# RWKV-7 scan: triangular inverses from 16 x 16 blocks on GpSimd and two block levels on TensorE, in place of 32 x 32 blocks and one level

## The chip, the core and the metric

One core of a Trainium2 chip runs the whole program in one launch. The metric is the device time of one execution in microseconds; the kernel before was executed three times.

## What is computed

The program is a two-layer trunk over 512 latent and 256 context tokens of width 1024. Layer 0 is half-SwiGLU, HGRN2 mixer, half-SwiGLU; layer 1 is half-SwiGLU, RWKV-7 mixer, half-SwiGLU; a final RMSNorm ends it. The change is in the RWKV-7 mixer of layer 1, in the scan over tokens. The reference, cut to that scan:

```
def rwkv_scan(decay, k, v, kk, b, r, s0, reverse):        # 16 heads of 64, two directions
    def step(s, inp):
        dec, kt, vt, kkt, bt = inp[:5]
        sa = einsum('bhvk,bhk->bhv', s, kkt)
        s = s * dec[:, :, None, :] - sa[..., None] * bt[:, :, None, :] + vt[..., None] * kt[:, :, None, :]
        y = einsum('bhvk,bhk->bhv', s, inp[5]) if with_out else None
        return s, y
```

Context tokens come first in each direction, and the latent scan starts from the final context state of the same direction.

## The kernel before, in words

`rwkv_scan(l)` (L1180) works in chunks of 64 tokens. In a chunk the recurrence becomes (I + A) U = right-hand side with a strictly triangular 64 x 64 matrix A for each head and direction, so each chunk needs the inverse Y of I + A; then come the products with U. A **group** is four heads (two channel tiles `e`, the half `hp` of each), both directions `d`, four chunks: 32 matrices of 64 x 64. There are 4 quads of heads times 3 groups (one of context, two of latent tokens), 12 in all, in the list `todo`.

For a group these generators write the instructions:

- `prep_a` (L1224) loads the features, makes the decays, forms A by products on TensorE (L1303), masks it on VectorE into `N` (L1309), transposes the backward one (`NT_`, L1314), and writes the diagonal blocks of 32 x 32 to a DRAM tile `md`, 8 DMAs on SyncE's queue (L1317): four from `N`, four from `NT_`.
- `prep_m` (L1322) loads `md` by GpSimd's queue so that each of 64 partitions holds one block (L1329), inverts all 64 blocks at once in 30 steps of two operations on GpSimd, a product into `mt` (L1335) and a sum into `M` (L1336), sets the diagonal (L1338) and writes the DRAM tile `me` (L1339).
- `prep_d` (L1343) reads `me` back into `P1`, blocks at their place in 64 columns, 8 DMAs on SyncE's queue (L1349).
- `prep_b` (L1351) turns k and b to tokens-major and forms A V (`bkt`, `W`).
- `prep_c` (L1385) transposes `P1` (L1390, two operations on VectorE) and forms the one off-diagonal 32 x 32 block of each matrix by two products of 32 x 32, `TT` (L1408) and `Yo` (L1410), with an eviction between them (L1413) and four copies behind (L1420, L1422).
- `scan` (L1429) runs the four chunks one after the other: `kG`, `rhs`, `U`, `VU`, `G`, and `y` on latent groups. `readout` (L1496) closes a quad.

Each matrix product of float32 shows as two MATMUL rows in the trace.

While group i is scanned, the loop at the end writes into the same stream the steps of `prep_a` of group i+2, of `prep_d`, `prep_b` and `prep_c` of group i+1, and of the inversions, at rates per step of the scan (`RP`, `RM`, `RO`). `SEQ = 'Adabc'` sets the order: two steps of `prep_a`, then `prep_d`, then the rest of `prep_a`, then b and c:

```
parts = {"A": islice(ahead, 2), "a": ahead, "b": stage(prep_b, i + 1), "c": ..., "d": urgent(stage(prep_d, i + 1), HP[2])}
prep = chain(*(parts[x] for x in SEQ))
for _ in urgent(scan(*k, *ready.pop(k)), HP[0]):
    for n, (f, r) in enumerate(((inversions, RM), (prep, RP), (out, RO))):
```

A scheduler then fixes the order on each engine and on each queue from an estimate of the times, with priorities from `urgent`; on the chip each engine and SyncE's queue go in that order and wait for what is not there yet. Tiles of 1024 floats come from two rotating sets, `Q` (L1191): 13 for `KR`, `BK`, `Ar`, 15 (`NQ2`) for the rest, `M` among them. PSUM banks come from `bank` (L1197).

Of the kernel before, what the change touches and what calls it, by code (L numbers as in the profile page):

```python
# [26 lines left out]
NQ1, NQ2 = 13, 15  # L27
RM, RP, RO, RV, RF = 3.0, 5.0, 0.3, 1.5, 1.3
# [25 lines left out]
# columns of the packed per-channel vectors  # L54
# [14 lines left out]
NCST = 790  # L69
# [4 lines left out]
def trunk(ctx, tc, io, phases=None, dump=None):  # L74
# [58 lines left out]

    def urgent(gen, by):
        """the steps of gen, their instructions ahead of others that wait"""
# [7 lines left out]
    def both(*gens):  # L143
        """the steps of all, in turns"""
# [31 lines left out]
    def wunit(src, nk, n=128, lo_on=None, keep=False):  # L176
        """[nk*128, n] of DRAM (or several, side by side) -> two parts whose sum it is, [128, nk, n] each"""
# [18 lines left out]
    def weights(todo, depth=None):  # L196
        """the units of todo in turn, those after them on their way"""
# [12 lines left out]
    def mm3_steps(p, w, c0, xs, n, cols=None):  # L210
        """p[:, :n] = (whi+wlo)[:, k, c0:c0+128]^T (xhi+xlo)[:, :n], summed over k; cols: (from, to, where in p) of other columns"""
# [31 lines left out]
    def mod_steps(l, s, ws=None, alloc=psmall):  # L243
        """part s of 9: [128, tile 8, (lat, ctx)]"""
# [32 lines left out]
    def rsqrt(p, n, scale, eps, lowest=None):  # L277
        """(scale*p + eps)^-0.5 of the n columns of p, to float32's accuracy"""
# [17 lines left out]
    def spread(ys, n, alloc=psum):  # L296
        """[128 tokens, chunk] -> the tokens along the free axis, on every partition (PSUM)"""
# [5 lines left out]
    def sums(x, n):  # L303
        """sum over the partitions of x[:, t] -> PSUM [128 tokens, chunk]"""
# [5 lines left out]
    def square(j, n, acc):  # L310
        """acc + h_j^2"""
# [15 lines left out]
    def norm_steps(l, sub, rs, out):  # L327
        """the modulated norm of h, in two parts, a tile at a time"""
# [80 lines left out]
        # sh, its upper half less its lower one, in two parts, and zeros  # L409
# [87 lines left out]
    def ffn(l, w, n, prep, fill=iter(()), rate=0.5):  # L497
        """prep: what is left of blocks' steps; fill: other work for the tensor engine, rate steps of it per unit of weights.
        Stops before the last rows; the steps that remain are two for each tile of the residual."""
# [44 lines left out]
        def columns(f):  # L544
            """g of the tile f"""
# [47 lines left out]
        def rows(f0, gs):  # L593
            """the residual from the tiles f0.. of g"""
# [41 lines left out]
    def hand_over(rest, prep):  # L636
        """the last rows of an FFN; what comes next prepares from each tile of the residual as it is done"""
# [10 lines left out]
    def lower_bound():  # L648
        """(lb, 1-lb): [128, dir*8+head]; softmax over the layers, of which there is one"""
# [13 lines left out]
    def hgrn(l, extra, after, u1, parts, cols, normed):  # L663
        """extra: for each head, parts of the modulation to work out on the way; after: steps to take as the residual's
        tiles are done"""
# [35 lines left out]
        def project(hd, first=False):  # L701
            F = pair("F")      # [bwd, fwd]
# [74 lines left out]
    def hgrn_head(hd, F, K2, qa, vals, ys):  # L777
# [35 lines left out]
        # products of the decays of blocks of 2, 4, ... 128 tokens  # L813
# [42 lines left out]
        # states at the head of each chunk  # L856
# [53 lines left out]
    def rwkv_dense(l, xpool, root):  # L910
        """all but the values that comes before the scan, per token; results go to DRAM"""
# [23 lines left out]
        def neighbour(j):  # L935
            """neighbour less token"""
# [25 lines left out]
        def mix_halves(m, n, out, low):  # L962
            """two steps for each tile"""
# [14 lines left out]
        def products(n):  # L978
            """n tiles for products; of one bank, there are the others"""
# [6 lines left out]
        def part(out, w, x, k, nk=NT):  # L986
            """the share of the input tile k in a product: out, a list of (PSUM, columns of the weights, from, to)"""
# [5 lines left out]
        # the first half of r and the hidden layers of a and of the decay, an input tile at a time: they come in one by one  # L993
# [78 lines left out]
        def features():  # L1072
            for j in range(NT):
# [49 lines left out]
                # output gate  # L1123
# [5 lines left out]
                # input of the values  # L1129
# [632 lines left out]
```

## Time and profile before

| what | value |
|---|---|
| three executions | 3957.18, 3948.7, 3953.75 us (median 3953.75) |
| span of the profiled execution | 3956.9 us (of the three executions the nearest took 3957.18 us) |
| TensorE busy | 3574.5 us, 90% |
| VectorE busy | 2687.5 us, 68% |
| ScalarE busy | 1454.9 us, 37% |
| GpSimd busy | 1424.3 us, 36% |
| granted TensorE clock, mean | 0.922 |

How to read it: TensorE is busy for 90% of the whole, but the share is a mean over stages. Clock 1.0 in a row is 2.4 GHz, 0.5 is 1.2 GHz, and a number between them is a mean over a stretch that had both. "PE" is TensorE's products, "DVE" VectorE, "ACT" ScalarE, "POOL" GpSimd, "SPq" SyncE's DMA queue. Times in rows are from the start of the span. A row's bracket tells how long the engine sat idle before it and what ended the wait.

### The profile page before, as it was taken

What the parts mean: (1) busy time and instruction counts of PE and PEld (TensorE: products, weight loads), DVE (VectorE), ACT (ScalarE), POOL (GpSimd) and SP (SyncE); (2) the same over time, 40 slices, a digit from 0 to 9 for tenths busy, and PEclk for the clock granted to TensorE, in tenths of its full rate; (3) what the DMA queues carried; (4) which work ended last, traced back from release to release, by engine and by line L of the source; (5) the groups of instructions that cost most, each with busy time, mean ns of one, the idle gap of its engine ahead of it and who ended that gap; (6) DMA issues with size and microseconds to landing.
All of it is one profiled execution on the core that took longest, in us unless ns stands there. A gap on an engine that the chain in (4) does not pass through costs nothing. (4 is left out here: it accounts for less than half of the span.)

```text
span 3956.9 us, 62237 instructions
## 1 busy us (share of the span) xinstructions
PE 3574.5 (90%) x24898; PEld 3201.7 (81%) x24898; DVE 2687.5 (68%) x4187; ACT 1454.9 (37%) x2168; POOL 1424.3 (36%) x1395
## 2 busy tenths in 40 slices
PE   4999999799999799999899999689878888888998
PEld 3999997688888699999799999566767776668887
DVE  7777676766576777767777677677444554468886
ACT  5433333432333544333533333344322222234343
POOL 3222223343343421222422222522356766623332
PEclk7999999999999899999999999799967777779999
DMA  5333232321111233333233222247632332232332
GB/s 162 107 96 101 86 91 64 89 61 41 41 49 38 59 106 114 107 102 107 64 94 91 83 89 90 64 133 228 189 92 69 90 84 66 60 104 82 98 93 80
DMA packets 517056, 362.56 MB, mean 92 GB/s; under 512 B 83517, under 2 KB 490333, under 8 KB 516766
## 3 DMA queue, kind: packets, MB, share of 16 engines
q1 hardware_dynamic: 513694, 350.19, 30.3%
q0 software_dynamic: 1920, 6.29, 0.6%
q8 instruction: 196, 3.21, 0.4%
q10 hardware_dynamic: 1152, 2.10, 0.2%
q14 instruction: 94, 0.77, 0.1%
HBM read 315.64 MB, written 42.87 MB: 91 GB/s over the span
## 5 line engine op out<-in xcount | busy, mean ns | idle before, releaser
L550 POOL TENSOR_TENSOR raw<-raw 128x512 f32<-128x512 f32 x88 | 132.5, 1506 | 1406.7 <-DMA raw<-in_ffn_w_in 797.8
L606 PE MATMUL po<-g,whi 128*128 128x512 f32 (+1 forms) x2464 | 585.3, 348 | 6.6 <-ACT g L207 4.0
L533 PE MATMUL c<-u,whi 128*128 128x386 f32 (+1 forms) x2112 | 521.9, 331 | 59.6 <-DVE uu L564 18.1
L192 ACT ACTIVATE whi<-raw 128x1024 fp32r<-128x1024 f32 (+1 forms) x337 | 335.0, 1000 | 401.8 <-PE po L606 122.8
L525 ACT ACTIVATE whi<-raw 128x1024 fp32r<-128x1024 f32 x352 | 330.6, 949 | 413.1 <-PE po L606 151.9
L526 DVE TENSOR_TENSOR wlo<-raw,whi 128x1024 fp32r<-128x1024 f32 x352 | 424.9, 1217 | 75.4 <-ACT whi L525 28.9
L606 PEld LDWEIGHTS po<-g,whi 128*128 128x128 f32 x2464 | 402.6, 189 | 69.9 <-ACT g L207 4.8
L533 PEld LDWEIGHTS c<-u,whi 128*128 128x128 f32 x2112 | 371.6, 190 | 74.5 <-ACT u L445 31.2
L193 DVE TENSOR_TENSOR wlo<-raw,whi 128x1024 fp32r<-128x1024 f32 (+1 forms) x289 | 358.8, 1248 | 57.8 <-ACT whi L192 56.4
L533 PE MATMUL a<-u,whi 128*128 128x386 f32 (+1 forms) x1408 | 349.3, 331 | 24.3 <-DVE u L427 14.8
L606 PE MATMUL po<-g,wlo 128*128 128x512 f32 (+1 forms) x1232 | 361.4, 347 | 0.0
L610 DVE SCALAR_TENSOR_TENSOR h<-po,mod,h 128x512 f32<-128x512 f32 (+1 forms) x384 | 226.9, 627 | 189.5 <-PE po L606 189.2
L533 PE MATMUL b<-u,whi 128*128 128x386 f32 (+1 forms) x1408 | 343.2, 328 | 3.5 <-ACT pp L561 2.2
L533 PE MATMUL c<-u,wlo 128*128 128x386 f32 (+1 forms) x1056 | 344.5, 326 | 0.0
L533 PEld LDWEIGHTS a<-u,whi 128*128 128x128 f32 x1408 | 252.1, 193 | 28.6 <-DVE u L427 15.3
L533 PEld LDWEIGHTS b<-u,whi 128*128 128x128 f32 x1408 | 246.2, 190 | 6.3 <-ACT pp L561 3.0
L533 PE MATMUL b<-u,wlo 128*128 128x386 f32 (+1 forms) x704 | 229.9, 327 | 4.2 <-DVE wlo L526 4.1
L533 PE MATMUL a<-u,wlo 128*128 128x386 f32 (+1 forms) x704 | 232.5, 330 | 0.5 <-DVE wlo L526 0.5
L606 PEld LDWEIGHTS po<-g,wlo 128*128 128x128 f32 x1232 | 205.9, 189 | 30.3 <-DVE wlo L193 0.2
L193 POOL TENSOR_TENSOR wlo<-raw,whi 128x1024 fp32r<-128x1024 f32 x48 | 126.4, 2634 | 278.6 <-ACT whi L192 269.3
L1335 POOL TENSOR_TENSOR mt<-M 64x168 f32<-64x168 f32 (+5 forms) x360 | 191.2, 532 | 66.9 <-DMA M<-md 34.7
L1336 POOL TENSOR_TENSOR M<-M,mt 64x168 f32<-64x168 f32 (+5 forms) x360 | 200.4, 557 | 26.4
(365 smaller groups left out, 7607.9 us busy)
## 6 DMA issues: line engine op xcount, KB each, us to landing
raw<-in_ffn_w_in SPq DMA_DIRECT2D x176, 512.0 KB
raw<-in_mod_w SPq DMA_DIRECT2D x144, 512.0 KB
raw<-in_ffn_w_out SPq DMA_DIRECT2D x80, 384.0 KB
raw<-in_hgrn_w_in SPq DMA_DIRECT2D x40, 512.0 KB
raw<-in_ffn_w_out SPq DMA_DIRECT2D x28, 512.0 KB
raw<-in_w_rkv SPq DMA_DIRECT2D x24, 512.0 KB
ld<-s_bk SPq DMA_DIRECT2D x48, 256.0 KB
s_bk<-knb SPq DMA_DIRECT2D x32, 192.0 KB
```

The lines of the kernel that those rows point to most:

```text
L192: act.activation(hi[:, :m], raw[:, :m], AF.Copy)
L193: (lo_on or slots["lo"]).tensor_tensor(lo[:, :m], raw[:, :m], hi[:, :m].bitcast(F32), ALU.subtract)
L525: act.activation(hi, x, AF.Copy)
L526: dve.tensor_tensor(lo, x, hi.bitcast(F32), ALU.subtract)
L533: pe.matmul(p[:, :q], a[:, c], x[k][:, b], start=first and k == 0 and i == 0, stop=k == 3 and i == 2, skip_group_check=not first)
L550: pool.tensor_tensor(S[:, lo], U[:, lo], U[:, hi], ALU.add)
L606: pe.matmul(p[v][:, :t1 - t0], wx[:, k, at:at + 128], x[:, e, t0:t1], start=k == 0 and i == 0, stop=k == nk - 1 and i == 2)
L610: dve.scalar_tensor_tensor(h[d][:, t0:t1], p[v][:, :t1 - t0], mods[l, sub, 2][:, d, v:v + 1], h[d][:, t0:t1], ALU.mult, ALU.add)
L1335: eng.tensor_tensor(t, M[:, 0:j, j:j + 1].to_broadcast([64, j, n]), M[:, j:j + 1, j + 1:32].to_broadcast([64, j, n]), ALU.mult)
L1336: eng.tensor_tensor(M[:, 0:j, j + 1:32], M[:, 0:j, j + 1:32], t, ALU.add)
```

## The change: what it does

The diagonal blocks become 16 x 16, so a group has 128 of them and fills 128 partitions; the inversion has 14 steps in place of 30. The blocks come back into `X` ([128, 2, 2, 8, 32]), a compact layout of 32 columns. `prep_c` gets a level more: with `T16` and `R16`, 64 products of 32 x 32 each, it makes 32 x 32 inverses from 16 x 16 ones, the old level follows on `A` and its transpose `AT`, and the result stands in `Y`. A mask `off16` comes with the constants. The steps of the inversions per step of the scan go from 3.0 to 1.5, `NQ2` from 15 to 14. Comments are taken out elsewhere. The core of the diff:

```diff
-NQ1, NQ2 = 13, 15
-RM, RP, RO, RV, RF = 3.0, 5.0, 0.3, 1.5, 1.3
+NQ1, NQ2 = 13, 14
+RM, RP, RO, RV, RF = 1.5, 5.0, 0.3, 1.5, 1.3
...
-        diagonal = [[B1.tile([128, 16, 64], F32, name=f"P1_{i}{d}") for d in range(2)] for i in range(2)]
+        diagonal = [B1.tile([128, 2, 2, 8, 32], F32, name=f"X16_{i}") for i in range(2)]
+        whole = [B1.tile([128, 2, 8, 64], F32, name=f"Y_{i}") for i in range(2)]
...
-        lanes = [(d, hp, b, d * 32 + (hp * 2 + b) * 8, 64 * hp + 32 * b) for d in range(2) for hp in range(2) for b in range(2)]
+        lanes = [(d, hp, b, d * 64 + (hp * 4 + b) * 8, 64 * hp + 16 * b) for d in range(2) for hp in range(2) for b in range(4)]
...
             for d, hp, b, l0, r0 in lanes:
                 nc.sync.dma_start(out=md[l0:l0 + 8].rearrange("l s t -> s l t"),
-                                  in_=(N[0] if d == 0 else NT_)[r0:r0 + 32, 8 * hp:8 * hp + 8, 32 * b:32 * b + 32])
+                                  in_=(N[0] if d == 0 else NT_)[r0:r0 + 16, 8 * hp:8 * hp + 8, 16 * b:16 * b + 16])
...
-            M = Q("M")[0:64, :1024].rearrange("l (s t) -> l s t", t=32)
+            M = B1.tile([128, 16, 16], F32, tag="M", name="M", bufs=2)
...
-            for j in range(30, 0, -1):
-                n = 31 - j
+            for j in range(14, 0, -1):
+                n = 15 - j
                 t = mt[:, :j * n].rearrange("l (a b) -> l a b", b=n)
-                eng.tensor_tensor(t, M[:, 0:j, j:j + 1].to_broadcast([64, j, n]), M[:, j:j + 1, j + 1:32].to_broadcast([64, j, n]), ALU.mult)
-                eng.tensor_tensor(M[:, 0:j, j + 1:32], M[:, 0:j, j + 1:32], t, ALU.add)
+                eng.tensor_tensor(t, M[:, 0:j, j:j + 1].to_broadcast([128, j, n]), M[:, j:j + 1, j + 1:16].to_broadcast([128, j, n]), ALU.mult)
+                eng.tensor_tensor(M[:, 0:j, j + 1:16], M[:, 0:j, j + 1:16], t, ALU.add)
...
             for d, hp, b, l0, r0 in lanes:
-                nc.sync.dma_start(out=P1[d][r0:r0 + 32, 8 * hp:8 * hp + 8, 32 * b:32 * b + 32], in_=me[l0:l0 + 8].rearrange("l s t -> s l t"))
+                o = 16 * (b % 2)
+                nc.sync.dma_start(out=X[r0:r0 + 16, d, d, :, o:o + 16], in_=me[l0:l0 + 8].rearrange("l s t -> s l t"))
...
-            for d in range(2):
-                dve.transpose(PT[d], P1[d][:, :, :32 + 32 * d])
+            for d in range(2):
+                dve.transpose(X[:, 1 - d, d].rearrange("p s n -> p (s n)"), X[:, d, d].rearrange("p s n -> p (s n)"))
...
+            p = view(bank("T16"))
+            for d in range(2):
+                for c in range(8):
+                    for hp, b, a in rows32:
+                        pe.matmul(p[a:a + 32, d, c], N[d][a:a + 32, 8 * hp + c, 32 * b:32 * b + 32], X[a:a + 32, 1, d, c], start=True, stop=True, tile_position=(a, a))
+                yield
+            dve.tensor_tensor(t16.rearrange("p d s n -> p (d s) n"), p.rearrange("p d s n -> p (d s) n"), off16.unsqueeze(1).to_broadcast([128, 16, 32]), ALU.mult)
+            p = view(bank("R16"))
+            for d in range(2):
+                for c in range(8):
+                    for hp, b, a in rows32:
+                        pe.matmul(p[a:a + 32, d, c], t16[a:a + 32, d, c], X[a:a + 32, 0, d, c], start=True, stop=True, tile_position=(a, a))
+                yield
+            A, AT = tile_of("A32"), tile_of("AT32")
+            dve.tensor_tensor(flat(A), flat(X[:, 0]), flat(p), ALU.add)
+            dve.transpose(flat(AT), flat(A))
+            for hp, b, a in rows32:
+                act.activation(Y[a:a + 32, :, :, 32 * b:32 * b + 32], A[a:a + 32], AF.Copy)
...
-                                    other = (PT[0] if d == 0 else P1[1])[a:a + 32, s, ca:ca + 32]
-                                    pe.matmul(pt[b:b + 32, lo:lo + 32], N[d][a:a + 32, s, cb_:cb_ + 32], other, start=True, stop=True, tile_position=(a, b))
+                                pe.matmul(pt[b:b + 32, lo:lo + 32], N[d][a:a + 32, 8 * hp + c, 32 * (1 - d):32 * (1 - d) + 32], AT[a:a + 32, d, c], start=True, stop=True, tile_position=(a, b))
...
-                        pe.matmul(p[half(hp), at(d, e)], Y[d][half(hp), slot(hp, e, cs[d])], rhs[half(hp), at(d, e)], start=True, stop=True)
+                        pe.matmul(p[half(hp), at(d, e)], Y[half(hp), d, 4 * e + cs[d]], rhs[half(hp), at(d, e)], start=True, stop=True)
```

## Rows read from the trace of the kernel before

**Rows 1.** The page's chain that ended last, over the whole run: shares of the span by engine.

```profile
PE 14%; POOL 4%; DVE 3%; DMA 1%; issue 1%; ACT 0%; SPq 0%; POOLq 0%; ACTq 0%; DVEq 0%
```

**Rows 2.** Busy time in the stretch of the scan's loop. Columns: from:to, length, then PE, PEld, DVE, ACT, POOL busy us (instructions), granted clock, DMA share, GB/s.

```profile
2870.00:3440.00 570.00, 476.10 (x6473) 402.25 (x6471) 270.05 (x601) 141.31 (x340) 369.42 (x695) 0.74 0.30 76
```

**Rows 3.** GpSimd's instructions in order of time: its loads of the blocks, the write of the inverses, the first of the 60 operations between them, and a pair of them.

```profile
2903.75 0.52 POOL L1329 DMA_DIRECT2D M<-md  x1 [32.58 <-PE Yo L1410]
...
2992.04 0.52 POOL L1329 DMA_DIRECT2D M<-md  x1 [10.12 <-DMA hw_s<-s_hw]
...
3301.36 0.52 POOL L1329 DMA_DIRECT2D M<-md  x1 [9.45 <-ACT Ei L1266]
3305.00 0.26 POOL L1335 TENSOR_TENSOR mt<-M 64x30 f32<-64x30 f32 x1 [3.12 <-DMA M<-md]
3305.34 0.26 POOL L1336 TENSOR_TENSOR M<-M,mt 64x30 f32<-64x30 f32 x1
...
3342.68 0.59 POOL L1339 DMA_DIRECT2D me<-M  x1 [0.29 <-POOL M L1336]
3353.18 0.52 POOL L1329 DMA_DIRECT2D M<-md  x1 [9.91 <-DMA md<-NT]
3398.38 0.52 POOL L1329 DMA_DIRECT2D M<-md  x1 [3.00 <-PE kG L1446]
```

**Rows 4.** SyncE's queue in order of time in the same turn, issue time of so many DMAs.

```profile
3345.60 3.75 SPq L1349 DMA_DIRECT2D P<-me  x8
3349.45 1.88 SPq L1317 DMA_DIRECT2D md<-NT  x4
```

**Rows 5.** The longest waits of SyncE's queue from 2870 to 3500: us in total, times, longest.

```profile
SPq L1349 <- DMA me<-M: 142.6, 12, 30.5
SPq L1242 <- PE y L1483: 49.0, 5, 15.9
```

**Rows 6.** Busy time from one load of blocks to the next, groups 3 to 11 (columns as in rows 2; the last row is the sum).

```profile
3045.26:3088.29 43.03, 42.43 (x603) 34.97 (x600) 23.10 (x53) 13.14 (x33) 33.69 (x64) 0.80 0.33 90
3088.29:3142.30 54.01, 42.41 (x534) 35.60 (x530) 25.00 (x56) 11.09 (x27) 33.83 (x63) 0.66 0.33 79
...
sum 406.34, PE 350.28 PEld 293.23 DVE 208.36 ACT 104.51 POOL 271.76; mean PE 43.79 PEld 36.65 DVE 26.05 ACT 13.06 POOL 33.97
```

**Rows 7.** Waits from 2870 to 3500, of VectorE and of TensorE: us in total, times, longest; and TensorE's two waits for the first transpose with their places.

```profile
DVE PT L1390 <- DMA P<-me: 89.7, 13, 15.9
...
PE TT L1408 <- DVE PT L1390: 25.1, 4, 13.1
PE U L1455 <- DVE rhs L1448: 14.1, 10, 5.5
...
PE cum L1263 <- DVE sg L1254: 7.7, 1, 7.7
PE sw L1250 <- DVE Ar L1309: 7.1, 1, 7.1
...
2956.91 0.31 PE L1408 MATMUL TT<-PT,N 32*32 32x32 f32 x4 [13.06 <-DVE PT L1390]
...
3403.56 0.32 PE L1408 MATMUL TT<-PT,N 32*32 32x32 f32 x4 [5.83 <-DVE PT L1390]
```

**Rows 8.** GpSimd's operations by shape, 3000 to 3040: busy us, mean ns of one, idle before.

```profile
L1335 POOL TENSOR_TENSOR mt<-M 64x240 f32<-64x240 f32 x2 | 1.6, 776 | 0.2
...
L1336 POOL TENSOR_TENSOR M<-M,mt 64x58 f32<-64x58 f32 x1 | 0.3, 279 | 0.0
L1335 POOL TENSOR_TENSOR mt<-M 64x30 f32<-64x30 f32 x1 | 0.2, 230 | 0.1
```

**Rows 9.** Pieces of the chain (start us, us, what) with the 32 x 32 products: a piece between others, an unbroken run at full clock, one at half clock; then the busy time of the instructions of `TT`, and of `Yo`, in the stretch of groups 3 to 11 (columns as in rows 2, engines that have none left out: PE, PEld and ACT for `TT`).

```profile
3360.84 0.17 PE TT L1408 x2
...
3364.26 0.70 PE Yo L1410 x50
...
3448.84 1.08 PE Yo L1410 x64
...
2992.04:3398.38 406.34, 17.61 (x512) 11.20 (x512) 3.07 (x8) 0.75 0.31 78
...
2992.04:3398.38 406.34, 10.88 (x512) 8.34 (x512) 6.61 (x16) 6.02 (x16) 0.75 0.31 78
```

**Rows 10.** Operations of VectorE and ScalarE by shape, 2992 to 3399: busy us, mean ns of one, idle before.

```profile
L1390 DVE STREAM_TRANSPOSE PT<-P 128x1024 f32<-128x1024 f32 x8 | 9.9, 1237 | 0.0
...
L1390 DVE STREAM_TRANSPOSE PT<-P 128x512 f32<-128x512 f32 x7 | 5.0, 711 | 50.9 <-DMA P<-me 50.9
...
L1507 DVE SCALAR_TENSOR_TENSOR ybuf<-mean,ybuf 128x512 f32<-128x512 f32 x5 | 3.4, 681 | 1.0 <-PE mean L1506 1.0
...
L1367 ACT ACTIVATE BKT<-bkt 128x512 f32<-128x512 f32 x33 | 19.0, 598 | 13.6 <-PE bkt L294 10.0 <-POOL M L1336 3.4
```

**Rows 11.** Busy time and granted clock in stretches of 4 us (columns as in rows 2).

```profile
3184.00:3188.00 4.00, 0.00 (x0) 0.00 (x0) 0.00 (x0) 0.00 (x0) 0.00 (x0) 0.89 0.40 81
3188.00:3192.00 4.00, 1.48 (x4) 1.19 (x5) 2.98 (x6) 0.00 (x0) 0.00 (x0) 0.50 0.33 51
...
3204.00:3208.00 4.00, 4.00 (x72) 3.08 (x72) 1.91 (x9) 0.00 (x0) 3.45 (x8) 0.95 0.00 0
3208.00:3212.00 4.00, 4.00 (x63) 3.28 (x63) 0.42 (x1) 0.50 (x2) 3.53 (x7) 0.50 0.02 4
```

More of the change, by code (lines that the diff above doesn't have):

```diff
@@ L68 @@
 NV = V_C + 16
-NCST = 790
+NCST = 822
 @with_exitstack
@@ L1210, in decay_weights @@
             nc.sync.dma_start(out=w2[64:65], in_=io["w0"][:, 256 * qd:256 * qd + 256].unsqueeze(0))
-        diagonal = [[B1.tile([128, 16, 64], F32, name=f"P1_{i}{d}") for d in range(2)] for i in range(2)]
-        for d in range(2):
-            dve.memset(diagonal[0][d], 0.0)
-            pool.memset(diagonal[1][d], 0.0)
+        diagonal = [B1.tile([128, 2, 2, 8, 32], F32, name=f"X16_{i}") for i in range(2)]
+        whole = [B1.tile([128, 2, 8, 64], F32, name=f"Y_{i}") for i in range(2)]
+        for x in diagonal:
+            dve.memset(x, 0.0)
+        for x in whole:
+            pool.memset(x, 0.0)
         FE, ME = dve, pool
@@ L1386, in prep_c @@
             KR, N, Ar, BKT, VU, W, gt, gs = ready[qd, g]
-            P1 = inverse.pop((qd, g))
-            PT = [late["B2"].tile([128, 16, 32], F32, tag="PT0", name="PT0", bufs=1), Q("PT").rearrange("p (s n) -> p s n", n=64)]
+            X = inverse.pop((qd, g))
+            Y = whole[(3 * qd + g) % 2]
             for d in range(2):
-                dve.transpose(PT[d], P1[d][:, :, :32 + 32 * d])
-                yield
-            Y = [P1[0], PT[1]]
+                dve.transpose(X[:, 1 - d, d].rearrange("p s n -> p (s n)"), X[:, d, d].rearrange("p s n -> p (s n)"))
+            yield
+            tile_of = lambda name: late["B2"].tile([128, 2, 8, 32], F32, tag=name, name=name, bufs=1)
+            view = lambda p: p.rearrange("p (d s n) -> p d s n", d=2, s=8)
+            flat = lambda x: x.rearrange("p d s n -> p (d s n)")
+            rows32 = [(hp, b, 64 * hp + 32 * b) for hp in range(2) for b in range(2)]
+            t16 = tile_of("t16")
+            p = view(bank("T16"))
[3 more added lines that the diff above has]
+                        pe.matmul(p[a:a + 32, d, c], N[d][a:a + 32, 8 * hp + c, 32 * b:32 * b + 32], X[a:a + 32, 1, d, c], start=True, stop=True, tile_position=(a, a))
+                yield
+            dve.tensor_tensor(t16.rearrange("p d s n -> p (d s) n"), p.rearrange("p d s n -> p (d s) n"), off16.unsqueeze(1).to_broadcast([128, 16, 32]), ALU.mult)
[10 more added lines that the diff above has]
+                act.activation(Y[a:a + 32, :, :, 32 * b:32 * b + 32], A[a:a + 32], AF.Copy)
+            yield
             tt = late["B2"].tile([128, 256], F32, tag="tt", name="tt", bufs=1)
@@ L1396, in prep_c @@
             for stage in range(2):
-                for e in range(2):
-                    for c in range(4):
-                        for d in range(2):
-                            for hp in range(2):
-                                s = slot(hp, e, c)
-                                lo = 32 * (s % 8)
-                                a = 64 * hp + 32 * d
-                                b = 64 * hp + 32 * (1 - d)
-                                ca, cb_ = 32 * d, 32 * (1 - d)
-                                if stage == 0:
-                                    other = (PT[0] if d == 0 else P1[1])[a:a + 32, s, ca:ca + 32]
-                                    pe.matmul(pt[b:b + 32, lo:lo + 32], N[d][a:a + 32, s, cb_:cb_ + 32], other, start=True, stop=True, tile_position=(a, b))
-                                else:
-                                    pe.matmul(py[a:a + 32, lo:lo + 32], tt[b:b + 32, lo:lo + 32], Y[d][b:b + 32, s, cb_:cb_ + 32], start=True, stop=True, tile_position=(b, a))
-                    yield
+                for c in range(8):
+                    for d in range(2):
+                        for hp in range(2):
+                            lo = 32 * c
+                            a = 64 * hp + 32 * d
+                            b = 64 * hp + 32 * (1 - d)
+                            if stage == 0:
+                                pe.matmul(pt[b:b + 32, lo:lo + 32], N[d][a:a + 32, 8 * hp + c, 32 * (1 - d):32 * (1 - d) + 32], AT[a:a + 32, d, c], start=True, stop=True, tile_position=(a, b))
+                            else:
+                                pe.matmul(py[a:a + 32, lo:lo + 32], tt[b:b + 32, lo:lo + 32], A[b:b + 32, d, c], start=True, stop=True, tile_position=(b, a))
+                    if c % 4 == 3:
+                        yield
                 if stage == 0:
```

14 lines of the change are left out of this document (8 added, 6 removed).

## The prediction

> **What bounds the kernel now.** I read the chain first. Over the whole run GpSimd has 4% of it, a share that only the scan can give, for the inversions are GpSimd's only work there [rows 1]. The scan's loop is 570 us long; TensorE is busy for 476 of them, at a mean clock of 0.74 [rows 2]. So two things compete: a loop through GpSimd, and TensorE's own work.
>
> The turns of the loop show which one sets the pace. From one load of blocks to the next in group order, groups 3 to 11 start at 2992.04 and 3398.38 [rows 3]: 406.3 us for eight turns, 50.8 each. Take the turn from 3301.36 to 3353.18. The load takes 3.6, the 60 operations and what is between them 37.7, the write of the inverses to its landing 2.9, then SyncE issues eight reads in 3.75 and, behind them in the same queue, four block writes of the *next* group in 1.9; 1.85 later the next load starts [rows 3, 4]. That is 51.8, the whole turn. The link is SyncE's order: the writes from `NT_` of group i+2 stand behind the reads of `me` of group i+1, which wait for GpSimd; the queue stood 142.6 us in twelve such waits [rows 5]. So the inversions run one after the other although groups are independent. VectorE stands in its own order behind the same landing (89.7 us), and TensorE catches it from VectorE: `TT`, `cum` and `sw` wait 25.1, 7.7 and 7.1 [rows 7].
>
> But TensorE is not far behind. In the eight turns it is busy for 43.8 of 50.8, idle for 7.0. One turn, 3045 to 3088, ran with 42.4 busy of 43.0 [rows 6]: that is how short a turn has been with TensorE packed.
>
> **The change, part by part.**
>
> *GpSimd.* 60 operations become 28, of 14 to 56 elements on 128 partitions. Operations of 30 and 58 elements take 0.23 and 0.28 [rows 8], with 0.08 between two starts and ends [rows 3]: 28 x 0.31 to 28 x 0.36, 8.7 to 10; I take 9.3 for 37.7. That twice the partitions double the time no row excludes; then it is 18.
>
> *SyncE's queue.* Reads and writes of blocks go from 8 to 16 each. At 0.47 for one [rows 4] the reads take 7.5 and the eight writes from `NT_` 3.8. Issue cost of a DMA with half the rows could be less; I keep 0.47. The loads of features, of `VU` and of the readout in the same queue come up to 3.75 later behind the reads and as much behind the writes; they are hidden as long as the queue has its 142.6 us of waiting to give. The new loop: 3.6 + 9.3 + 2.9 + 7.5 + 3.8 + 1.85 = 29 us, 38 with GpSimd doubled. Either is under TensorE's time, so the loop through GpSimd stops deciding. `M` in tiles of its own and one slot fewer in the rotating set cost nothing: eight of 15 per group become six of 14.
>
> *TensorE.* `T16` and `R16` are 128 products a group, 256 rows of the trace. The nearest rows are those of `Yo`, the same size, on four tiles in turn: 50 in 0.70 us at full clock, 64 in 1.08 at half [rows 9], 14 and 17 ns each: 3.6 to 4.3 us. `TT`, broken up by the scan's products, has 17.6 us for 512, 34 ns: 8.8 us. A piece of two between others costs 0.17, which for all would be 22; the new products are written 64 rows at a time, so that end is not reached. I take 4.3, with 3.6 and 8.8 as ends.
>
> The Trainium skill speaks against this price: TensorE: Matmul & The Clock Gate, "Wait — 56ns, not 53.3ns?", has successive matmuls never start less than about 25 ns apart, however small. The rows of `Yo` are below it, on tiles side by side. By the page's 25 ns the 256 rows would take an estimated 6.4 us, and the sum below would end near 3942 instead.
>
> *VectorE and ScalarE.* Two transposes of 1.95 together go [rows 10]. Two of 256 columns come (0.45 each along the line through 0.71 at 512 and 1.24 at 1024), the masked eviction and the sum at about 0.68 each (the row of 128x512 out of PSUM), and a transpose of 512 at 0.71: 3.0, so 1.0 more. VectorE has 26 busy of 50.8 [rows 6] and hides it. ScalarE gets four copies of 512 columns, 4 x 0.6 = 2.4 [rows 10], beside 13 busy; one ahead of `VU` could hold the scan for 0.6, which I put at nothing because the copies come before the group's scan.
>
> *Latency of `prep_c`.* T16, eviction, R16, sum and transpose add 1.1 + 0.7 + 1.1 + 0.7 + 0.7 = 4.3 before `TT`. In the loop the inverses land some 20 us earlier, which covers it; only for the first group, where `prep_c` runs ahead of the scan, it may show: 0 to 4.3, I take 2. The banks of PSUM used in turn by `bkt`, `W`, `TT` and `Yo` get two more users; their cost is in the upper end.
>
> *The sum.* In the loop a turn becomes that of TensorE packed, 43.0, plus 4.3 = 47.3, against 50.8: 3.5 x 8 = 28 us. I take the packed turn and not the mean of 43.8, because the waits that go also leave stretches at half clock behind them [rows 11]. Ahead of these turns the 13.06 us in which TensorE waits for the second group's transpose goes, against two groups' new products, 8.6: 4.5. At the end the wait of 5.8 goes [rows 7] and some 3 where the last inverses land, against 4.3: 4.5. Less the 2: 35 us. The profiled execution's span is 3956.9, 3.2 above the median of the three runs, so I take the difference from the median: 3953.75 - 35 = 3919. What a measurement can tell from no change is 0.2%, 8 us.
>
> What is late next: `kG`, `U` and `G` of the scan, one after the other through VectorE and ScalarE, in TensorE's order between everybody else's products.
>
> **Rivals.**
>
> *TensorE becomes the bound, and slower (0.15).* If the new products are dealt out among the scan's as those of `TT` are, they cost 8.8 a group, and with the mean turn's work it is 43.8 + 8.8 + 0.6 = 53.2: 2.4 x 8 = 19 us lost, 4.6 at the front (17.6 - 13.06), nothing at the end, 2 for the first group: about 3980. It decides from 6.4 us of new products a turn on, 25 ns each. For it: `prep_c` is `urgent` like the scan, so the two mix. Against it: `Yo`, equally urgent, runs in long pieces.
>
> *The clock comes up (0.20).* After the idle time from 3184 the granted clock is 0.5 [rows 11]; with the waits gone TensorE might stay higher. At 0.9 instead of the packed turn's 0.80 [rows 6], 42.4 would be 37.7; with 3.8 of new products and 0.6 idle it is 42.1, a gain of 8.7 x 8 + 7 = 77: 3877. Against it: the clock also fell at 3208, where TensorE had been busy for all of the 4 us before, in a stretch with the 32 x 32 products [rows 11], and these become three times as many.
>
> The Trainium skill has a rule for it, TensorE: Matmul & The Clock Gate, "What's actually happening": recent busyness of TensorE sets the clock. By it a packed scan would keep full clock; the first of the two falls agrees with it, the second does not.
>
> *Another wait takes the loop's place, no change (0.13).* The second-direction load of `KR` waits for the scan's last `y`: SyncE stood 49.0 us in five waits on that line alone [rows 5]. If that fixes the turn near 50, or if the inversions are no shorter than before, only the ends remain: 3945 to 3955. Against it: with the features free at a scan's end, the chain from there to the inverses is shorter by the same 28 us.
>
> **How the numbers follow.** The likeliest case, 0.52, gives 3919, and by its own bounds (3.6 to 6.4 us of new products, first group 0 to 4.3) 3905 to 3942. Faster by over 0.2%: 0.50 of it, the clock's 0.20 and 0.01 of the third, 0.71. Within 0.2%: 0.02 and 0.12, 0.14. Slower: 0.15. The range of 3868 to 3962 takes in the clock's case but for its far end, the whole of the unchanged one, and the mild part of the slower one.
>
> **What would show it.** GpSimd's time from load to write near 9 to 10 us a group; SyncE's waits for `me` far under 142.6; VectorE's for the reads' landing gone; turns of 46 to 49 us with TensorE busy for over 95%; `T16` and `R16` together 3.6 to 5 us a group. It would be wrong if the turns stay at 50 with TensorE idle (another loop), if `T16` and `R16` take over 6.4 us, or if the clock in the loop leaves 0.70 to 0.80.

## The result and the profile after

The changed kernel took 4004.3 us (median of four runs, 3999.4 to 4010.1) beside 3953.7 of the kernel before: a ratio of 1.0129, 95% interval 1.0114 to 1.0144. That is 51 us slower where 35 us of gain were forecast. Up to 2800 us both profiles agree within 3 us of TensorE's busy time (2572.3 and 2569.4); from the first `U` product to the last the scan grew from 573.4 to 624.4 us, and that is the whole loss.

The chain that ended last, by engine. It answers to [rows 1]:

```profile
PE 22%; DVE 5%; DMA 2%; SPq 2%; POOL 1%; issue 1%; ACT 1%; ACTq 0%; DVEq 0%; POOLq 0%
```

GpSimd's share fell from 4% to 1%, and TensorE's rose from 14% to 22%, more than GpSimd gave up; VectorE, the DMAs and SyncE's queue rose by one or two points each.

Busy time in the scan's loop and in the eight turns, groups 3 to 11, with the columns of [rows 2, 6]:

```profile
2870.00:3440.00 570.00, 527.79 (x8672) 439.99 (x8670) 234.35 (x603) 155.87 (x355) 90.30 (x314) 0.75 0.25 64
...
2983.32:3437.26 453.94, 432.64 (x6991) 357.02 (x6993) 187.93 (x491) 122.54 (x281) 71.94 (x249) 0.74 0.24 62
```

A turn is 56.7 us (453.94 / 8) with TensorE busy for 54.1; before it was 50.8 with 43.8. Idle time fell from 7.0 to 2.7 as it should, and 10.3 us of work came. The clock did not move.

GpSimd in one turn, in order of time (start, us, what), against [rows 3]:

```profile
3095.98 0.54 POOL L1334 DMA_DIRECT2D M<-md  x1 [36.44 <-DMA hw_s<-s_hw]
3098.83 0.29 POOL L1340 TENSOR_TENSOR mt<-M 128x14 f32<-128x14 f32 x1 [2.31 <-DMA M<-md]
...
3108.81 0.58 POOL L1344 DMA_DIRECT2D me<-M  x1 [0.30 <-POOL M L1341]
...
3151.37 0.54 POOL L1334 DMA_DIRECT2D M<-md  x1 [41.98 <-DMA KR<-s_kk]
```

From the first operation to the write it is 10.0 us (forecast 9.3, before 37.7): twice the partitions did not double the time. GpSimd then stands idle for 42 us: the eight block writes of the next group are issued from 3143.65 on, after VectorE's transpose into `NT` behind TensorE's `A`, and the row names the landing of a feature load issued just behind them. SyncE's queue in the same turn, against [rows 4]:

```profile
3112.05 8.59 SPq L1355 DMA_DIRECT2D X<-me  x16
...
3143.65 3.64 SPq L1322 DMA_DIRECT2D md<-NT  x8
```

16 reads take 8.6 (forecast 7.5), eight writes 3.6 (3.8). The loop through GpSimd is as short as forecast; TensorE's part is not. Its instructions by shape in the eight turns (count, busy us, mean ns of one, idle before):

```profile
L1409 PE MATMUL T<-X,N 32*32 32x32 f32 x1143 | 55.5, 216 | 0.5 <-issue 0.5
L1493 PE MATMUL G<-VU,BKT 128*64 128x64 f32 x480 | 51.4, 258 | 1.0 <-ACT VU L1487 0.8
...
L1416 PE MATMUL R<-X,t 32*32 32x32 f32 x1024 | 26.8, 238 | 0.3 <-DVE t L1411 0.2
```

`T16` takes 49 ns a row (55.5 / 1143) and `R16` 26; the forecast had 14 to 17. The same 480 rows of `G` took this before, groups 3 to 11:

```profile
L1465 PE MATMUL G<-VU,BKT 128*64 128x64 f32 x480 | 34.4, 261 | 0.2 <-ACT VU L1459 0.2
```

51.4 against 34.4, though the mean of one instruction is the same: the rows are not longer, they overlap less. The timeline of TensorE shows between what (start, us, rows in a piece); the granted clock is 1.00 here, 2.4 GHz:

```profile
3099.71 0.75 PE L1409 MATMUL T<-X,N 32*32 32x32 f32 x64
3100.39 0.33 PE L1483 MATMUL U<-rhs,Y 64*64 64x64 f32 x4
3100.65 0.24 PE L1409 MATMUL T<-X,N 32*32 32x32 f32 x2
3100.83 0.33 PE L1483 MATMUL U<-rhs,Y 64*64 64x64 f32 x2
3101.08 0.24 PE L1409 MATMUL T<-X,N 32*32 32x32 f32 x2
3101.26 0.33 PE L1483 MATMUL U<-rhs,Y 64*64 64x64 f32 x2
3101.51 0.24 PE L1409 MATMUL T<-X,N 32*32 32x32 f32 x2
```

64 rows of `T16` on end go from 3099.71 to the next start at 3100.39, 11 ns each. Then they are dealt out, two and two, among the scan's 64 x 64 products: from one pair of `U` to the next is 0.43 us (3100.83 to 3101.26). With 0.02 for the two small rows and under 0.07 for the two of `U`, as they would take on end, some 0.34 to 0.40 is left for two changes of kind: **0.17 to 0.20 us a change**, at full clock. By the starts of the single rows, 0.148 lies between the last `U` and the first `T16` and 0.121 on the way back; the rest lies between the two rows of a pair (0.107 and 0.052), which on end overlap with others. Counted in the order of TensorE's program, from the first 32 x 32 product to the last, there are 184 such changes before and 582 after. The Trainium skill bears on it: TensorEngine Tiling (Array Packing), "Key Properties", says that changing the tiling mode drains TensorE. The 0.43 us agree with it; no run here shows the drain by itself.

### The profile page after: what moved, and what is told of

Same layout as the page of the kernel before. It is cut to its first block, busy times and chain, and to the rows that moved or that the text cites. A ratio compares the mean times of both kernels' runs of the same rounds, so it can differ in the third digit from the quotient of the medians.

```text
span 4004.0 us, 68242 instructions
## 1 busy us (share of the span) xinstructions
PE 3671.0 (92%) x27970; PEld 3275.4 (82%) x27970; DVE 2661.7 (66%) x4223; ACT 1484.4 (37%) x2216; POOL 1121.1 (28%) x1011
## 5 line engine op out<-in xcount | busy, mean ns | idle before, releaser
L533 PEld LDWEIGHTS c<-u,wlo 128*128 128x128 f32 x1056 | 202.0, 191 | 0.0
L252 PE MATMUL modp<-whi,cb 128*32 128x256 f32 x576 | 151.7, 291 | 19.6 <-ACT whi L192 19.6
```

What stands on the lines that cost most here:

```text
L252: pe.matmul(p[0:32, 0:256], st, w[i][:, k, :], start=(j == 0 and k0 + k == 0 and i == 0), stop=(j == 3 and k0 + k == 7 and i == 1))
L533: pe.matmul(p[:, :q], a[:, c], x[k][:, b], start=first and k == 0 and i == 0, stop=k == 3 and i == 2, skip_group_check=not first)
```

## The experiments

Four explanations stood against each other: the **change-overs** between 32 x 32 products and others; the **volume** of the new products; another **wait**, SyncE's in-order reads of the inverses above all; and a lower granted **clock**. All times are medians, beside runs of the kernel before on the same chip; "changes" are those just counted. The last three columns come from the profiles, from the first `U` to the last: I add up the time from each MATMUL's start to the next one's, set apart what lies between an end and the next start, and give the mean granted clock. (One turn in the scan varies too much from group to group to compare kernels by.)

| run | us | ratio to before [95%] | changes | TensorE's work | its gaps | clock |
|---|---|---|---|---|---|---|
| before | 3953.7 | | 184 | 477 | 96 | 0.74 |
| after | 4004.3 | 1.0129 [1.0114, 1.0144] | 582 | 570 | 54 | 0.73 |
| a_noT | 3942.6 | 0.9977 [0.9962, 0.9992] | 170 | 484 | 85 | 0.74 |
| b_8 | 3943.7 | 0.9970 [0.9948, 0.9992] | 206 | 526 | 56 | 0.70 |
| a_hp | 3991.4 | 1.0105 [1.0085, 1.0124] | 106 | 481 | 121 | 0.75 |
| a_pe | 3983.8 | 1.0073 [1.0058, 1.0088] | 94 | 473 | 132 | 0.77 |
| a_pool | 4009.2 | 1.0143 [1.0122, 1.0163] | 560 | 571 | 50 | 0.72 |
| a_pepool | 3942.1 | 0.9978 [0.9965, 0.9990] | 94 | 469 | 93 | 0.81 |
| a_hppool | 3967.6 | 1.0041 [1.0026, 1.0056] | 104 | 484 | 86 | 0.76 |
| a_noT_pepool | 3894.5 | 0.9856 [0.9841, 0.9870] | 46 | 466 | 62 | 0.75 |
| b_hp | 3953.9 | 1.0003 [0.9992, 1.0013] | 62 | 452 | 128 | 0.75 |
| b_pepool | 3954.2 | 1.0007 [0.9998, 1.0017] | 46 | 424 | 156 | 0.78 |
| b_hppool | 3947.4 | 0.9984 [0.9975, 0.9994] | 58 | 458 | 123 | 0.72 |
| b8_hp | 3877.4 | 0.9809 [0.9789, 0.9829] | 52 | 434 | 79 | 0.81 |
| b_dum | 4061.3 | 1.0270 [1.0254, 1.0287] | 356 | 554 | 118 | 0.70 |
| b8_dum_hp | 3989.3 | 1.0095 [1.0080, 1.0110] | 90 | 514 | 85 | 0.73 |
| b8_vol_hp | 3962.9 | 1.0025 [1.0012, 1.0038] | 98 | 505 | 76 | 0.74 |
| b8_trip_hp | 3908.7 | 0.9892 [0.9875, 0.9908] | 88 | 464 | 70 | 0.76 |

### The new products left out: a_noT

The kernel after without `T16` and `R16`; the two operations behind them on VectorE read another tile.

```
-  pe.matmul(p[...], N[d][...], X[a:a + 32, 1, d, c], ..., tile_position=(a, a))    # T16, and the same for R16
-  dve.tensor_tensor(t16, p, off16, ALU.mult)
+  dve.tensor_tensor(t16, X[:, 0], off16, ALU.mult)
```

> The changed kernel with the products T16 and R16 left out (the masked copy and the sum read the blocks themselves in their place, so the inverses lack one level); 582 changes of kind become 170. This is the forecast of the prediction without its price of new products: the sum by its steps is 3953.75 - 35 - 8 turns x 4.3 - 9, about 3875 to 3885. Theory 'changing over': the whole loss and more comes back, 3870 to 3905. Theory 'another wait' (a queue or slots hold the turn): 3970 to 4004, TensorE idle for over 5 us a turn.

3942.6: the products cost 62 us (forecast some 47, 4.3 for each of 11 groups), and all else in the change gains only 11. The forecast without the products' price would have been a gain of 82. This is the larger error: with inversions of 10 us and no new products the eight turns still took 50.0 us each with TensorE busy for 43.9 in the windows view, the same work as before:

```profile
2973.96:3373.74 399.78, 350.90 (x4935) 298.80 (x4934) 187.35 (x494) 124.58 (x289) 76.70 (x248) 0.78 0.28 70
```

Neither expected range was met. TensorE's 6.1 us of idle time a turn are the sign of the third theory, another wait. SyncE still stood 110.0 us for the inverses, but so it did in b8_hp (108.6), the fastest run below; which wait holds the turn is not shown.

### Only the inversion shorter: b_8

The kernel before with 8 of the inversion's 30 steps; the other 22 are left out.

```
-  for j in range(30, 0, -1):
+  for j in range(8, 0, -1):
```

> The kernel before with 8 of the 30 inversion steps kept (the others left out, so the inverses are not whole): 16 operations on GpSimd, about 8 us a group in place of 37, no new product; 206 changes of kind. Theory 'loop through GpSimd bound the kernel before': turns of 43 to 46 us, 3880 to 3920. Theory 'TensorE already bound it': within 10 us of 3954.

3943.7, 10 us gained, about what "TensorE already bound it" expected; the packed turn had promised more. Its eight turns:

```profile
2964.90:3390.54 425.64, 393.68 (x4994) 328.67 (x4996) 186.13 (x471) 103.90 (x257) 65.05 (x153) 0.72 0.29 75
```

TensorE is indeed packed now, its gaps down from 96 to 56 us. But the turn is 53.2 us, not 43: the same products take 49.2 us of it instead of 43.8. The one short turn of [rows 6] was no measure of what a packed loop would do. By the profiles the scan is even 8 us longer than before, 581 against 573, and what was gained lies ahead of its first `U`. From the first `U` to the last (columns as in [rows 2], before and b_8):

```profile
2907.20:3480.40 573.20, 477.07 (x6593) 401.24 (x6592) 274.04 (x617) 139.23 (x337) 368.08 (x692) 0.74 0.29 73
2896.30:3477.70 581.40, 525.59 (x6593) 438.70 (x6592) 243.80 (x618) 137.44 (x337) 89.43 (x208) 0.70 0.28 73
```

The same rows took 49 us more, at a lower granted clock. I sort the steps from one MATMUL's start to the next by their two shapes and by the clock, and give each sort its mean price in the two traces; by this estimate 26 of the 49 us come from the clock, the rest from the order. The clock also moves the time of one and the same program: nine of b_8's ten executions took 3932.7 to 3950.7 (the profiled one) at a mean clock over the whole run of 0.919 to 0.924, and one 3908.5 at 0.935.

### Before, with the small products grouped: b_hp, b8_hp

`prep_c` and `prep_d` are ranked further ahead of the scan, so that the scheduler writes their 32 x 32 products in long runs (an expectation that ranks the scan lower means this edit). b8_hp has b_8's edit as well.

```
-  HP = 800, 400, 800
+  HP = 800, 400, 1600
```

> The kernel before with the same raised priority, 184 changes of kind to 62. Theory 'changing over' with the loop through GpSimd as the bound: 61 round trips at 0.35 are 21 us of TensorE's time, of which the loop lets little through: 3935 to 3955. Theory 'order alone' (the raised priority is good for any kernel, whatever its 32x32 products): a gain near that of the changed kernel with it, 60 us or more: under 3900.

> The kernel before with 8 of the 30 inversion steps kept (the others left out, so the inverses are not whole) and the raised priority: 52 changes of kind in place of 206, no wait for GpSimd. Each alone moved the time by 0 to 9 us: the raised priority took 25 us of TensorE's work off and the loop through GpSimd turned them into waits; the short inversion took 40 us of waits off and TensorE's work grew by 48. Theory 'two bounds beside each other': both together give work of 452 us and waits of 55, a scan of about 510, time 3885 to 3905. Theory 'the scan's own chain': 3940 to 3955.

b_hp: no difference. TensorE's work falls by 25 us, near 122 fewer changes at 0.17 to 0.20 (21 to 24), and its gaps grow by 32, because GpSimd's 38 us still set the turn. b8_hp: 76 us faster than before, and below the 3885 to 3905 expected of two bounds. Shorter inversions alone gave 10, grouping alone 0, both 76. Its turns:

```profile
2964.29:3319.76 355.47, 310.05 (x4878) 265.15 (x4878) 183.47 (x470) 103.79 (x255) 66.14 (x152) 0.86 0.36 90
```

44.4 us a turn with 38.8 busy, at 0.86. Here is the packed turn of the forecast, but it took an order of TensorE's program that neither kernel has, and a higher clock: of the 91 us by which TensorE's work is below that of b_8, some 65 come from the clock (estimated as above), and the rest from the order.

### After, with the small products grouped, and the reads on another queue: a_hp, a_pe, a_pool, a_pepool, a_hppool

a_hp has the edit of `HP`. a_pe ranks only the four kinds of 32 x 32 product ahead, a_pool moves the reads of `me` from SyncE's queue to GpSimd's; a_pepool has both of these, a_hppool `HP` and the queue.

```
+  with tc.high_priority(offset=800):                                            # a_pe
       pe.matmul(..., tile_position=(a, a))                                      # T16, R16, TT, Yo

-  nc.sync.dma_start(out=X[r0:r0 + 16, d, d, :, o:o + 16], in_=me[...])
+  pool.dma_start(out=X[r0:r0 + 16, d, d, :, o:o + 16], in_=me[...])             # a_pool
```

> The changed kernel with one number changed: the priority of prep_c and prep_d is raised, so that the scheduler writes the 32x32 products in long runs. The same products, but in TensorE's order the changes between a 32x32 product and another kind fall from 582 to 106 (the kernel before has 184). Theory 'changing over': a pair of 32x32 rows between two rows of 64x64 has a turn of 0.43 us where unbroken runs of the two would take about 0.12, so a round trip costs 0.3 to 0.45; 238 round trips fewer at 0.35 is 83 us: about 3921, at least 3960. Theory 'work': the 3072 rows more and the longer chain of prep_c cost what they cost in any order: 3990 to 4015. Theory 'clock': small products lower the granted clock: time near 4004 and the clock in the scan's loop no higher than 0.75.

> The changed kernel with a raised priority for the 32x32 products alone (T16, R16, TT, Yo), not for the DMAs, transposes and copies around them: 582 changes of kind become 94, the order of the other queues stays by its old priorities. In the run with the priority of all of prep_c raised, TensorE's work between the first and the last U fell from 570 to 481 us, but its waits grew from 54 to 121, VectorE standing 118 us for the reads of the blocks. Theory 'order': without that the waits stay near 60 to 80, so the scan takes 545 to 560 in place of 624: 3930 to 3950. Theory 'the scan's own chain' (no order of the products helps, time freed on TensorE comes back as waiting): 3980 to 4000.

> The changed kernel with the sixteen reads of the inverses issued on GpSimd's queue in place of SyncE's, and the priorities as they are: 560 changes of kind. Grouping the products alone gave 20 us (4004 to 3984), both edits together 62 (3942). Theory 'two bounds beside each other' (SyncE's order and TensorE's broken order): this one alone gives less than the missing 42, since TensorE's work stays at 570 us with waits of 54 already: 3980 to 4004. Theory 'SyncE's queue alone was the loss': 3955 to 3965.

> As the changed kernel with a raised priority for the 32x32 products alone, and the sixteen reads of the inverses issued on GpSimd's queue in place of SyncE's, so that the writes of the next group's blocks and the loads of features don't stand behind them. Theory 'SyncE's order is what comes next': 10 to 30 us below the run without it. Theory 'TensorE decides': within 8 us of it; a rival cost is that a DMA issued from GpSimd lands later, up to 10 us slower.

> The kernel after with the scan's instructions ranked lower as a whole (104 changes of kind in the program's order, against 582) and the reads of the inverses on GpSimd's queue. By the theory that change-overs and SyncE's order together hold the loop, it lands where the ranking of the small products alone did with the same queue: 3935 to 3950. If that kernel's 3942 hung on its particular order, it stays near 3991, where the ranking alone stood.

Grouping takes away 476 and 488 changes and 89 and 97 us of TensorE's work: 0.19 and 0.20 a change, and 0.18 and 0.16 without what the clock gave back (2 and 20 us, estimated as above), near the price read from the timeline. The steps over a change with no idle time in them add up to 99 us in the kernel after and 11 or 12 in these two. The time falls by only 13 and 21 us, because the gaps grow from 54 to 121 and 132; so a_hp landed where "work" had put it, and a_pe where "the scan's own chain" had. What stands in them is SyncE and VectorE behind the reads again, as in [rows 5, 7]. The waits of a_pe's SyncE (us in total, times, longest) and VectorE:

```profile
SPq L1355 <- DMA me<-M: 134.2, 11, 17.8
```

```profile
DVE X L1397 <- DMA X<-me: 129.8, 20, 12.8
```

In the kernel after these are 117.8 and 61.9, hidden by TensorE's work. The queue alone (a_pool) gains nothing, 5 us the other way; on top of a_pe it gains 42, more than the 10 to 30 expected. a_pepool at 3942.1 beats both kernels, the one before by 12 us. By shape, its small products in the eight turns:

```profile
L1410 PE MATMUL T<-X,N 32*32 32x32 f32 x1152 | 16.4, 193 | 2.5 <-issue 2.4
...
L1418 PE MATMUL R<-X,t 32*32 32x32 f32 x1071 | 13.1, 199 | 4.5 <-issue 3.7 <-DVE t L1412 0.7
```

14 and 12 ns a row, where the forecast took 14 to 17: **the unit price was right, for the order it assumed**. a_hppool, which differs from a_pepool in that all of `prep_c` and `prep_d` is ranked ahead and not the products alone, is 25 us slower at nearly the same number of changes, between its two expectations. Its granted clock is lower (0.76 against 0.81), and the order of the rest differs too; which of the two decides is not settled.

### The same two edits on the kernel before: b_pepool, b_hppool

> The kernel before, whole, with the raised priority for TT and Yo alone and the eight reads of the inverses issued on GpSimd's queue, so that the writes of the next group's blocks no longer stand behind them in SyncE's queue; 46 changes of kind. The loop is then GpSimd's own: load 3.6, inversion 37.7, 2.9 to the landing, eight issues of 0.55: 48.6 a turn, or 45 where the next load is already issued. Theory 'two bounds beside each other': 3900 to 3940. Theory 'no gain while GpSimd takes 45 us a turn': 3945 to 3960.

> The same with the raised priority for all of prep_c and prep_d in place of the products alone; 58 changes of kind. Expected within 15 us of the run with the products alone; the better of the two is the candidate against both kernels.

0 and 6 us gained, with gaps of 156 and 123: as long as the inversions take 38 us, neither TensorE's work nor SyncE's order decides. So what a_pepool and b8_hp gain is not a general gain of grouping; it needs the short inversions.

### What the products cost when grouped: b_dum, b8_dum_hp

256 rows of unused 32 x 32 products a group are added to `prep_c`, in two PSUM banks that a small copy on VectorE reads; b_dum is on the kernel before, b8_dum_hp on b8_hp.

```
+  for nm in ("T16", "R16"):
+      p = bank(nm)...
+      for d in range(2):
+          for c in range(8):
+              for hp, b, a in rows32:
+                  pe.matmul(p[a:a + 32, d, c], N[d][...], PT[0][...], start=True, stop=True, tile_position=(a, a))
+      dve.tensor_copy(xs, p[:, :, :, 0])
```

> The kernel before with 128 more 32x32 products a group, as many as the change adds, at the place of T16 and R16 in prep_c; their results are read into a tile that nobody uses; 356 changes of kind in place of 184. Theory 'the products are on the path' (TensorE decided the pace already before): 40 to 65 us slower, 3995 to 4015. Theory 'the idle time takes them' (the loop sets the pace, and TensorE has 7 us a turn to give): 3950 to 3968.

> The kernel before with 8 of the 30 inversion steps kept (the others left out, so the inverses are not whole), the raised priority, and 128 unused 32x32 products a group more at the place of T16 and R16; 90 changes of kind. Against 3877 without the products it prices them alone, in long runs, with no loop and only 8 reads: 3072 rows of the trace at 11 to 17 ns are 34 to 52 us of TensorE, so 3905 to 3935. If it is 3880 to 3890 the products are hidden, and the loss of the changed kernel is the DMAs and the chain of prep_c; if it is over 3950 the added steps in prep_c's chain cost more than the rows.

They cost 107 us on the kernel before and 112 on b8_hp, although the latter writes them in long runs: its 32 x 32 rows take 47.5 us of the scan, 11 ns each, 34 more than in b8_hp. Both are above all that was expected. So their price is three times their own time, and change-overs are not all of it: b8_dum_hp has only 38 more than b8_hp.

### Volume or round trip: b8_vol_hp, b8_trip_hp, a_noT_pepool

b8_vol_hp has the unused products and no copy behind them; b8_trip_hp has banks and copies, and eight rows of products for each bank instead of 128. (The 256 products of its expectations are rows, two for each product; b8_trip_hp has eight products a group.) a_noT_pepool is a_noT with the edits of a_pe and a_pool.

```
-      dve.tensor_copy(xs, p[:, :, :, 0])                          # b8_vol_hp

-      for d in range(2):                                          # b8_trip_hp
-          for c in range(8):
+      for d in range(1):
+          for c in range(1):
```

> The kernel before with eight of the inversion's 30 steps and the scan ranked lower (the kernel that took 3877), with the 256 unused 32x32 products a group, but nothing that reads them: nothing waits for their results. With the readers it took 3989, 112 more. By the theory that the products' own time on TensorE is the price, the whole of it comes without the readers too: 3975 to 3995. By the rival, that the price is the trip from TensorE to VectorE and back through the rotating banks, only the rows' time in long runs is left, 3072 x 11 ns = 34 us: 3905 to 3920.

> The same kernel with the two banks and their readers on VectorE, but eight unused products a group in place of 256. By the theory that the products' own time is the price: 3877 to 3885, as without them. By the rival, that the trip through banks and VectorE is the price: 3930 to 3960, that is 50 to 80 of the 112 us.

> The kernel after without the new products (their evictions read another tile), with the other 32x32 products ranked ahead of the scan on TensorE and the reads of the inverses on GpSimd's queue. With the products, the same took 3942. If the products cost what they did elsewhere (62 to 112), it is 3830 to 3880. If, grouped and with SyncE's order out of the way, they cost only their time on TensorE (34 to 37), it is 3905 to 3910. If without them another loop holds the scan, 3930 to 3942.

Against b8_hp the volume costs 85 us and the round trip 31; together 116, beside 112 for both. The first two expectations each missed: neither theory is alone. b8_vol_hp's turns:

```profile
2978.75:3405.81 427.06, 373.45 (x6954) 319.43 (x6954) 184.07 (x472) 104.61 (x259) 65.75 (x152) 0.77 0.30 76
```

The clock is 0.77 where b8_hp's was 0.86. Of its 67 us in the scan, 33 are the rows themselves, 37 are the *other* products, which take longer (from start to next start 70 ns instead of 64 for products on 64 rows, 111 instead of 102 on 128), and gaps give 3 back; another 23 lie ahead of the first `U`. b8_trip_hp has the same clock, 0.77; its other rows take 27 us longer, while the gaps are 9 shorter. The rotating banks are therefore not waited for: what both edits cost beyond their own rows is slower rows of others at a lower granted clock. Sorted by shapes and clock as for b_8, the clock makes 43 of the 70 us that b8_vol_hp's work grew, and 27 of b8_trip_hp's 30. Why the clock falls with eight small rows and a copy is not shown.

a_noT_pepool's 3894.5, between two of its expected ranges, is what the change without its products can reach with these two edits, 59 us under the kernel before; the products then cost 48 (a_pepool less a_noT_pepool), between the bare rows' 36 and the 62 of the kernel after.

## Why the prediction was wrong

**GpSimd and SyncE's issue times: right.** The inversion took 10.0 for 9.3, reads 8.6 for 7.5, writes 3.6 for 3.8. The loop through them no longer set the turn: TensorE had 2.7 us idle in 56.7. Two of the signs did not come all the same: SyncE's waits for `me` are 117.8 and not far under 142.6, and VectorE's for the reads are 61.9, before 89.7, and not gone.

**VectorE: of the wrong sign, without consequence.** It was to be busy for 1.0 us more a turn and was for 2.6 less (187.93 / 8 = 23.5, before 26.1), because many of its other operations became shorter when GpSimd's inversion did. The same 32 operations, before and after:

```profile
L1280 DVE TENSOR_TENSOR BK<-ld,Ei 128x512 f32<-128x512 f32 x32 | 29.2, 948 | 3.4 <-PE y L1483 3.2
L1285 DVE TENSOR_TENSOR BK<-ld,Ei 128x512 f32<-128x512 f32 x32 | 20.7, 686 | 5.8 <-PE bkt L294 5.2 <-PE y L1511 0.6
```

In b_8, which shortens the inversion alone, they take 695 ns.

**The step that failed is "a turn becomes that of TensorE packed, 43.0".** It took the shortest turn of the trace [rows 6] as what TensorE needs. b_8 and a_noT have the short inversion and none of the new products: 53.2 and 50.0 us a turn, and 10 and 11 us of gain in all, for the forecast's 82. That is 71 of the 85 us of error; the products are the rest. What took the place of the wait on GpSimd differs between the two. In b_8 it is TensorE's own work, which is no fixed amount: it rose from 43.8 to 49.2 us a turn, and by the estimate above about half of the rise in the scan is a lower granted clock. In a_noT it looks like another wait: TensorE works 43.9 and stands idle for 6.1, and grouping and the other queue together take 48 us off (a_noT_pepool); which of the two does it was not tried alone. The short turn was reached only with the 32 x 32 products kept together as well (b8_hp, 44.4), and at a clock of 0.86, where the forecast's short turn had 0.80.

**The price of the new products was too low for its place: 62 us instead of 47.** "The new products are written 64 rows at a time, so that end is not reached" was read from the source; the scheduler dealt them out two and two. The forecast had seen the sign of it, a piece of two between others at 0.17 us [rows 9], and had priced it as a dear product, not as two change-overs that also set the scan's products apart. In the eight turns they cost 6.7 us each (56.7 less a_noT's 50.0), and 10.2 of TensorE's busy time (54.1 less 43.9), above the 8.8 of the upper end. The forecast's bounds were also added up wrongly: its own terms give 3909 to 3944 for the likeliest case, not 3905 to 3942.

**The rivals.** "TensorE becomes the bound, and slower" came true, on its own condition: the new products passed 6.4 us a turn, dealt out as those of `TT` are; its price of 3980 was 24 short; that the scan's rows are spread as well, as those of `G` above, is in none of its terms. The argument against it, that `Yo` runs in long pieces at the same rank, did not carry over to products that stand beside a running scan. "The clock comes up" did not happen here (0.74), but b8_hp shows it exists, 0.86 and 3877; that this is the rival's number is chance, for b8_hp is another kernel, without the new products. The Trainium skill's rule, that recent busyness sets the clock (TensorE: Matmul & The Clock Gate, "What's actually happening"), would have put the clock up here: TensorE was busy for 95% of the eight turns at 0.74, and for 87% at 0.86 in b8_hp. The trace does not agree. Nor does it with the same page's floor of about 25 ns between matmuls ("Wait — 56ns, not 53.3ns?"): 64 rows on side-by-side tiles started 11 ns apart.

**Left open.** What makes the granted clock fall in the scan; it differs between orders of TensorE's work and, in b_8, between executions of one order, but the runs name no cause. And what holds a_noT's turn at 50 us.

## What to carry to other kernels

Work moved to TensorE is priced by where the scheduler puts it: here, small products on tiles cost 11 to 14 ns a row on end, and some 0.16 to 0.20 us for every change to another shape, twice that there and back, paid by their neighbours too; read the scheduled order before believing the source's. A wait that fills most of a loop may stand beside a second bound of nearly its length, and the shortest turn in a trace does not tell what is left without the wait; shorten the one engine's work by itself first, as b_8 does, and see. Compare the granted clock before crediting an edit: here it moved TensorE's work by as much as the edits did. When a loop has two or three such bounds, judge an edit in company: grouping was worth between 0 and 67 us and the other queue between 0 and 42, depending on what else had been done.

## What the runs showed of the hardware

- A change between 32 x 32 products and 64 x 64 ones cost TensorE 0.17 to 0.20 us at a granted clock of 1.00 by the timeline, and 0.16 to 0.18 at the scan's mix of clocks by the sum over 476 and 488 changes taken away, without what the clock gave back. In the scan of the kernel after, the first 32 x 32 row starts 0.148 us after the last 64 x 64 one at 1.00 and 0.241 at 0.50, and the first 64 x 64 row 0.121 and 0.166 after the last 32 x 32 one (medians).
- The change is not particular to 32 x 32: between 64 x 64 and 128 x 64 products the same starts lie 0.148 apart one way and 0.152 the other at 1.00.
- At a granted clock of 0.50 (1.2 GHz) a round trip, which took 0.43 us at 1.00, took 0.64, seen with `R16` and `kG` of the kernel after (start to start):

```profile
3106.70 0.31 PE L1416 MATMUL R<-X,t 32*32 32x32 f32 x2
3106.94 0.47 PE L1474 MATMUL kG<-G,KR 64*64 64x64 f32 x2
3107.34 0.31 PE L1416 MATMUL R<-X,t 32*32 32x32 f32 x2
```

- GpSimd's operation of 54 elements on 128 partitions took 0.29 us, that of 58 on 64 partitions 0.28 [rows 8], and all 28 took 10.0 with what is between them: twice the partitions did not show as time.
- A VectorE operation of 128x512 (`BK`, mean of 32) took 948 ns beside GpSimd's inversions of 38 us, and 686 (the kernel after) to 695 (b_8) beside the short ones.
